# Own buffers for the first chunk's raw weights, and a running sum made by accumulating DMAs, in a two-layer encoder

## The chip, the cores and the metric

The kernel runs on one core of a Trainium2 chip. The metric is the time of one launch on the device, in microseconds (us). Below, PE is TensorE, DVE is VectorE, ACT is ScalarE, POOL is GpSimd and SP is SyncE. SP issues the loads; an engine name with a q behind it (SPq) is that engine's queue of DMA issues.

## The reference

Two layers are run on one sequence of 256 tokens of width 2048. Each layer multiplies x by a wide matrix, gives the columns to four attention branches (A to D), and adds the branches up, each with its own gate:

```python
x = _layer_norm(x, emb_ln_g, emb_ln_b)
for l in range(DEPTH):                      # DEPTH = 2
    h = jnp.einsum('bsd,de->bse', x, w_in)  # q, k, v, z of four branches, and gl
    ...
    ys = jnp.stack([ya * jax.nn.silu(az), yb * jax.nn.silu(bz), yc * jax.nn.silu(cz), yd * jax.nn.silu(dz)], axis=2)
    proj = jnp.einsum('bsnw,nwd->bsnd', ys, w_branch)
    gates = jax.nn.sigmoid(gl + b_gate).reshape(b, s, N_BRANCH, D_MODEL)
    merged = jnp.sum(proj * gates, axis=2)
    out = jnp.einsum('bsd,de->bse', merged, w_out)
    x = _layer_norm(DN_ALPHA * x + out, ln_g, ln_b)
```

## The kernel before

**Tiling.** The 256 tokens are two halves of 128 partitions. Weights come as raw groups of 128 x 1024 fp32 (512 KB, two k-tiles of 512 columns) in tiles `wraw` of a pool of four. ACT rounds a group to `whi` (line 145) and DVE takes the rest, `wlo` (line 146). A chunk of 512 columns is eight groups: PE multiplies each group three times (low x by high w, high x by high w, high x by low w; lines 190, 191 and 194) into one PSUM bank for each half. `chunk_t` (lines 217 and 218) does the same with the weights as the stationary side.

**The order of the work.** Each engine runs its own list in order. A scheduler makes the lists from the program's order and the free tiles; inside `first_chunk` the order is written out by hand. A wait at the head of an engine's list holds everything behind it.

**The first chunk.** `first_chunk` overlaps the first layer norm with the first 512 columns. x is loaded into `merged`, normalized, transposed on PE (line 558), scaled by ACT into `xt` or `xt1` (line 561) and split by ACT and DVE into `tx` (lines 235 and 236). For half 0, PE multiplies `xt` by the raw weights (`plain`, line 595, four matmuls of fp32 for each c). For half 1 it uses the split ones: `split_pass(c)` (lines 602, 603 and 606) reads two groups and the four k-tiles of `tx` that `x1_t(c)` has made. The eight raw groups are called raw 0 to raw 7 here. Raws 4 to 7 are issued one by one, each when `split` has freed a tile of the pool. Groups 4 to 7 are split into borrowed tiles (`wsp`, by `SPARE`). Behind raw 7 SP issues nine small loads (`small_weights`: rope tables, masks, `lp`, `sg`, `gn`), and only then the raw groups of the next chunk.

**The sum over the branches.** `gates(b)` runs over four chunks c of 512 columns: the gate's columns, then `gt` and `g` (lines 824 and 826), then a projection chunk of four groups, and then, for each half, `gp` = (g + 1) x projection (line 839) and `merged += gp` (line 840), both on DVE. Branch 0 writes `merged` directly (line 836). Around the last projection chunk, (b, c) = (3, 3), PE transposes columns c = 0, 1 and 2 of `merged` (line 806, `merged_t`). Columns c = 3 follow in `merged_last`, a task that is stepped after the first group of the first `w_out` chunk. `merged_t` fills `tx` again, the left side of that matmul.

Of the kernel before, what the change touches and what calls it, by code (L numbers as in the profile page):

```python
# [11 lines left out]
F32 = mybir.dt.float32  # L12
F32R = mybir.dt.float32r
AF = mybir.ActivationFunctionType
ALU = mybir.AluOpType
AX = mybir.AxisListType

P = 128
# [4 lines left out]
NK = D // P  # L23
KG = 2
# [2 lines left out]
TCH = 256  # L27

SPARE = [None] * 4 + [(("qkT", 3), ("qkT", 3)), (("v", 2), ("v", 2)), (("ra", 1), ("rb", 1)), (("yl", 2), ("yl", 2))]
NCH = 512  # L30
WARM = 40
ALPHA = (2 * DEPTH) ** 0.25
# [60 lines left out]
def hybrid_encoder(ctx: ExitStack, tc: tile.TileContext, a: dict, out: bass.AP):  # L93
# [33 lines left out]
    def load_bc(dst, src_1d):  # L127
        nc.sync.dma_start(out=dst, in_=src_1d.rearrange("(o n) -> o n", o=1).to_broadcast([P, src_1d.shape[0]]))

    loads = []  # L130


    def load_raw(src, off, w):
        raw = wrw.tile([P, KG * NCH], F32, tag="wraw", name="wraw")[:, :w]
        loads.append(nc.sync.dma_start(out=raw, in_=src[off:off + P * w].rearrange("(p m) -> p m", p=P)).ins)
        return raw

# [94 lines left out]
    def split_evac(hi, lo, src, scale=None):  # L232

        if scale is None:
            nc.scalar.copy(hi, src)
            nc.vector.tensor_tensor(out=lo, in0=src, in1=hi.bitcast(F32), op=ALU.subtract)  # L236
        else:
            nc.scalar.activation(out=hi, in_=src, func=AF.Copy, scale=scale)
            nc.vector.scalar_tensor_tensor(out=lo, in0=src, scalar=scale, in1=hi.bitcast(F32), op0=ALU.mult, op1=ALU.subtract)
# [327 lines left out]
    def first_chunk(src, off):  # L567

        acc = acc_banks()
        xt = cst.tile([P, NK, P], F32, tag="bias", name="xt")  # L570
        size = P * KG * NCH
        raws, ws = [], []

        def load_raws(n):
            for _ in range(n):
                raws.append(load_raw(src, off + len(raws) * size, KG * NCH))

        def split(n):
            for _ in range(n):
                g = len(ws)  # L580
                ws.append(split_w(raws[g], NCH, SPARE[g]))
                if g + 4 < NK // KG:
                    load_raws(1)

        def x0_t(c):
            x_t(0, c, xt[:, 4 * c:4 * c + 4])

        def x1_t(c):
            t = vec.tile([P, 4, P], F32, tag="tmp", bufs=3, name="xt1")
            x_t(1, c, t)  # L590
            x_split(1, c, t)

        def plain(c):
            for k in range(4 * c, 4 * c + 4):
                nc.tensor.matmul(acc[0], lhsT=xt[:, k], rhs=raws[k // KG][:, k % KG * NCH:(k % KG + 1) * NCH], start=k == 0, stop=k == NK - 1)  # L595

        def split_pass(c):
            for g in (2 * c, 2 * c + 1):
                hi, lo = ws[g]
                for kk in range(KG):  # L600
                    k = g * KG + kk
                    nc.tensor.matmul(acc[1], lhsT=tok(tl, k, 1, False), rhs=hi[:, kk], start=k == 0, stop=False)
                    nc.tensor.matmul(acc[1], lhsT=tok(th, k, 1, False), rhs=hi[:, kk], start=False, stop=False)
                for kk in range(KG):
                    k = g * KG + kk
                    nc.tensor.matmul(acc[1], lhsT=tok(th, k, 1, False), rhs=lo[:, kk], start=False, stop=k == NK - 1)

        load_x(0)
        nc.scalar.dma_start(out=gT, in_=a["emb_ln_gT"])
        nc.scalar.dma_start(out=bT, in_=a["emb_ln_bT"])  # L610
        load_raws(2)
        load_x(1)
        load_raws(2)

        idle = psa.tile([P, NCH], F32, tag="pa", name="idle")
        for _ in range(WARM):
            nc.tensor.transpose(idle[:, :P], ident, ident)
        m0 = stats_of(0)
        for c in range(4):
            center(0, c, *m0)  # L620
        split(1)
        x0_t(0)
        x0_t(1)
        split(1)
        m1 = stats_of(1)
        plain(0)
        x0_t(2)
        split(1)
        plain(1)
        x0_t(3)  # L630
        split(1)
        plain(2)
        for c in range(4):
            center(1, c, *m1)
        split(1)
        x1_t(0)
        split(1)
        plain(3)
        x1_t(1)
        split(1)  # L640
        split_pass(0)
        split(1)
        x1_t(2)
        split_pass(1)
        x1_t(3)
        split_pass(2)
        x_split(0, 0, xt[:, 0:4])
        x_split(0, 1, xt[:, 4:8])
        split_pass(3)
        x_split(0, 2, xt[:, 8:12])  # L650
        x_split(0, 3, xt[:, 12:16])
        return acc
# [18 lines left out]
    for l in range(DEPTH):  # L671
# [51 lines left out]
        def columns_ab(br):  # L723
            zs, ysT = new_branch()
            for u in range(2):
                v = v_tile()
                first = (br, u) == ("A", 0)
                if first and l == 0:
                    with tc.manual_schedule(engines={mybir.EngineType.PE, mybir.EngineType.Activation, mybir.EngineType.DVE, mybir.EngineType.SP}):
                        ps = first_chunk(w_in, OFFSETS[f"{br}vz{u}"])  # L730
                else:
                    ps = cols(f"{br}vz{u}", apart=first)
                if not sw:
                    if l == 0:
                        with tc.issue_after(loads[-1]):
                            sw.extend(small_weights())
                    else:
                        sw.extend(small_weights())
                neglam, sg, gn, bias = sw
                for half in range(2):  # L740
                    nc.vector.tensor_copy(v[:, half, 0:256], ps[half][:, 0:256])
                    silu2(ps[half][:, 256:512], zs[:, half, u * 256:(u + 1) * 256], sg if br == "A" else None)
                hi, lo = qkT_tile(4), qkT_tile(4)
                for b in range(2):
                    bs = slice(b * NCH, (b + 1) * NCH)
                    ps = cols_t(f"{br}qk{u}", b)
                    src = att.tile([P, 1024], F32, tag="ra", name="xr", bufs=1)[:, :NCH]
                    fold(ps, src.rearrange("p (n t) -> p n t", n=2))
                    if br == "A":
                        table = [rope_a[:, i].rearrange("p (j m) -> p j m", j=2).unsqueeze(1).to_broadcast([P, 2, 2, P]) for i in range(2)]  # L750
                        rotate(src.rearrange("p (n j m) -> p n j m", n=2, j=2), P, *table)
                    split_evac(hi[:, bs], lo[:, bs], src)
                tasks.append(attend_a(u, (hi, lo), v, zs, ysT, neglam) if br == "A" else attend_b(u, (hi, lo), v, zs, ysT, bias))
            if br == "A" and l == 0:
                tasks.append(keep_x())
            return ysT
# [57 lines left out]
        def gates(b, ysT, first):  # L814
            yh, yl = ysT
            for c in range(4):
                cs = slice(c * NCH, (c + 1) * NCH)
                bg = vec.tile([P, NCH], F32, tag="bc", name="bg")
                load_bc(bg, a["b_gate"][l][b * D + c * NCH:b * D + (c + 1) * NCH])
                ps = cols(f"G{b}{c}")  # L820
                gs = []
                for half in range(2):
                    t = vec.tile([P, NCH], F32, tag="tmp", bufs=3, name="gt")
                    nc.vector.tensor_tensor(out=t, in0=ps[half], in1=bg, op=ALU.add)  # L824
                    g = vec.tile([P, NCH], F32, tag="g", bufs=3, name="g")
                    nc.scalar.activation(out=g, in_=t, func=AF.Tanh, scale=0.5)  # L826
                    gs.append(g)
                if c == 0:
                    drain_for(b)
                if (b, c) == (3, 3):  # L830
                    for done in range(3):
                        merged_t(done)
                pp = chunk(w_br, (b * 4 + c) * P * 4 * NCH, NCH, 4, yh, yl)
                for half in range(2):
                    if first:
                        nc.vector.scalar_tensor_tensor(out=merged[:, half, cs], in0=gs[half], scalar=1.0, in1=pp[half], op0=ALU.add, op1=ALU.mult)
                    else:
                        t = vec.tile([P, NCH], F32, tag="tmp", bufs=3, name="gp")
                        nc.vector.scalar_tensor_tensor(out=t, in0=gs[half], scalar=1.0, in1=pp[half], op0=ALU.add, op1=ALU.mult)
                        nc.vector.tensor_tensor(out=merged[:, half, cs], in0=merged[:, half, cs], in1=t, op=ALU.add)  # L840

        pending = {}

# [144 lines left out]
```

## Time and profile before

| what | value |
|---|---|
| time, median of 3 runs | 2127.93 us (2125.24 to 2128.4) |
| the profiled execution, its own time | 2127.32 us |
| its span, first to last instruction | 2125.2 us |
| granted PE clock, mean | 0.997 |
| PE busy | 2105.6 us, 99% |
| DVE, ACT, POOL busy | 1316.8, 997.9 and 33.7 us |
| DMA, bytes moved and mean rate | 410.38 MB, 193 GB/s |

The time holds 2.1 us around the span. A busy PE is counted from pipelined matmuls, so that 99% says that PE hardly ever waits, not that it is at its peak. A chain of waits through the program is 97% PE.

### The profile page before, as it was taken

The page shows a single profiled execution, that of the slowest core. Times are in us where ns is not written, and L with a number is a line of the kernel's source. Part 1 is how long each engine was busy: PE and PEld are TensorE (multiplying, and loading weights), DVE is VectorE, ACT ScalarE, POOL GpSimd, SP SyncE. Part 2 cuts the span into 40 slices and gives each one's busy share as a digit, 9 for nine tenths or more (in the row PEclk, how much of TensorE's full clock was granted, in tenths as well). Part 3 has the DMA queues.
Part 4 walks back from the last instruction along what each step waited for, and adds up shares of the span by engine and source line. Part 5 has one row for each costly group of instructions (what it writes and reads, how often), then busy time and mean ns, then how long its engine had stood idle before and what let it go on. Part 6 is the DMA issues. An engine that isn't in the chain of part 4 may idle for free.

```text
span 2125.2 us, 27271 instructions
## 1 busy us (share of the span) xinstructions
PE 2105.6 (99%) x10480; PEld 1787.3 (84%) x10480; DVE 1316.8 (62%) x1635; ACT 997.9 (47%) x1335; POOL 33.7 (2%) x34
## 2 busy tenths in 40 slices
PE   8999999999999999999999999999999999999997
PEld 6888888888898988888888888888889999888886
DVE  6767655765566655556676665556656666555566
ACT  5654444444455544444446544444445454444442
POOL 1000100000000000000000000000000000000000
PEclk9999999999999999999999999999999999999999
DMA  7557566556555566666665555665565555666664
GB/s 245 180 179 264 194 201 195 185 182 198 181 175 169 171 206 204 212 198 225 204 211 181 173 169 189 199 187 187 184 203 183 174 168 179 196 200 214 198 217 145
DMA packets 121457, 410.38 MB, mean 193 GB/s; under 512 B 13872, under 2 KB 14896, under 8 KB 120816
## 3 DMA queue, kind: packets, MB, share of 16 engines
q1 hardware_dynamic: 120464, 407.59, 59.8%
q8 instruction: 82, 1.34, 0.3%
q10 hardware_dynamic: 864, 1.07, 0.1%
q14 instruction: 47, 0.39, 0.1%
HBM read 402.31 MB, written 6.29 MB: 192 GB/s over the span
## 4 chain that ended last, share of the span: by engine, by line
PE 97%; DVE 1%; DMA 1%; ACT 0%; issue 0%; DVEq 0%; POOL 0%; SPq 0%
PE pw L190 23%; PE pw L191 23%; PE pw L194 23%; PE pw L217 14%; PE pw L218 7%; PE pt L291 1%; PE po L446 1%; PE po L518 1%; PE sc L504 1%; DMA wraw<-in_w_in 0%; PE pw L595 0%; DVE wlo L146 0%; PE sc L378 0%; PE pt L806 0%; PE po L401 0%; PE pt L338 0%
## 5 line engine op out<-in xcount | busy, mean ns | idle before, releaser
L146 DVE TENSOR_TENSOR wlo<-wraw,whi 128x1024 fp32r<-128x1024 f32 (+1 forms) x720 | 865.8, 1204 | 653.1 <-ACT whi L145 653.0
L145 ACT CAST whi<-wraw 128x1024 fp32r<-128x1024 f32 (+1 forms) x720 | 742.7, 1033 | 930.3 <-PE pw L191 686.5
L190 PE MATMUL pw<-whi,tx 128*128 128x512 f32 (+1 forms) x1968 | 760.7, 387 | 0.4 <-DVE tx L236 0.4
L191 PE MATMUL pw<-whi,tx 128*128 128x512 f32 (+1 forms) x1968 | 753.6, 383 | 0.0
L194 PE MATMUL pw<-wlo,tx 128*128 128x512 f32 (+1 forms) x1968 | 593.3, 383 | 0.0
L217 PE MATMUL pw<-tx,whi 128*128 128x512 f32 x1280 | 457.0, 400 | 0.0
L190 PEld LDWEIGHTS pw<-whi,tx 128*128 128x128 f32 x1968 | 371.6, 189 | 65.9 <-DVE tx L236 0.6
L191 PEld LDWEIGHTS pw<-whi,tx 128*128 128x128 f32 x1968 | 371.8, 189 | 64.3
L194 PEld LDWEIGHTS pw<-wlo,tx 128*128 128x128 f32 x1968 | 368.6, 189 | 68.0
L218 PE MATMUL pw<-tx,wlo 128*128 128x256 f32 x1280 | 358.4, 280 | 0.0
L217 PEld LDWEIGHTS pw<-tx,whi 128*128 128x128 f32 x1280 | 240.4, 188 | 56.2
L218 PEld LDWEIGHTS pw<-tx,wlo 128*128 128x128 f32 x1280 | 241.7, 189 | 0.5
L190 PE MATMUL pw<-whi,yl 128*128 128x512 f32 x256 | 100.8, 394 | 0.0
L191 PE MATMUL pw<-whi,yh 128*128 128x512 f32 x256 | 99.8, 390 | 0.0
L194 PE MATMUL pw<-wlo,yh 128*128 128x512 f32 x256 | 79.4, 390 | 0.0
L194 PEld LDWEIGHTS pw<-wlo,yh 128*128 128x128 f32 x256 | 48.1, 188 | 10.1
L190 PEld LDWEIGHTS pw<-whi,yl 128*128 128x128 f32 x256 | 48.1, 188 | 9.6
L191 PEld LDWEIGHTS pw<-whi,yh 128*128 128x128 f32 x256 | 48.1, 188 | 9.5
L824 DVE TENSOR_TENSOR gt<-pw,bg 128x512 f32<-128x512 f32 x64 | 44.0, 687 | 9.4 <-PE pw L194 9.4
L826 ACT ACTIVATE g<-gt 128x512 f32<-128x512 f32 x64 | 37.2, 623 | 7.7 <-DVE gt L824 7.7
L325 ACT COPY xs<-qkT 32x512 f32<-32x512 f32 x48 | 29.7, 619 | 23.5 <-DVE qkT L230 23.2
L226 ACT COPY fo<-pw 128x256 f32<-128x256 f32 x80 | 29.7, 371 | 17.4 <-PE pw L218 17.2
(151 smaller groups left out, 1109.0 us busy)
## 6 DMA issues: line engine op xcount, KB each, us to landing
wraw<-in_w_in SPq DMA_DIRECT2D x544, 512.0 KB, 3.9
wraw<-in_w_branch SPq DMA_DIRECT2D x64, 512.0 KB, 3.4
wraw<-in_w_out SPq DMA_DIRECT2D x64, 512.0 KB, 4.3
wraw<-in_w_in SPq DMA_DIRECT2D x64, 384.0 KB, 3.1
bg<-in_b_gate SPq DMA_DIRECT2D x32, 256.0 KB, 4.3
xr<-x_dram SPq DMA_DIRECT2D x16, 256.0 KB, 4.7
bias<-in_rpb SPq DMA_DIRECT2D x2, 1024.0 KB, 6.7
x_dram<-merged SPq DMA_DIRECT2D x8, 256.0 KB, 5.1
```

The costliest lines, as they stand in the source:

```text
L145: nc.scalar.copy(hi[:, :w], raw)
L146: nc.vector.tensor_tensor(out=lo[:, :w], in0=raw, in1=hi[:, :w].bitcast(F32), op=ALU.subtract)
L190: nc.tensor.matmul(acc[half][:, :n], lhsT=tok(ll, k, half, perm), rhs=hi[:, kk, :n], start=k == 0, stop=False)
L191: nc.tensor.matmul(acc[half][:, :n], lhsT=tok(lh, k, half, perm), rhs=hi[:, kk, :n], start=False, stop=False)
L194: nc.tensor.matmul(acc[half][:, :n], lhsT=tok(lh, k, half, perm), rhs=lo[:, kk, :n], start=False, stop=k == nkt - 1)
L217: nc.tensor.matmul(acc[b], lhsT=hi[:, kk, cs], rhs=tx[:, k].rearrange("p h t -> p (h t)"), start=k == 0, stop=False)
L218: nc.tensor.matmul(acc[b][:, SEQ:], lhsT=lo[:, kk, cs], rhs=th[:, k, :], start=False, stop=k == NK - 1)
L226: nc.scalar.copy(t[:, b], acc[b][:, :SEQ])
L291: nc.tensor.transpose(pt[:, q * P:(q + 1) * P], src[:, q * P:(q + 1) * P], ident)
L325: nc.scalar.copy(xs[r:r + 32], x[r ^ 32:(r ^ 32) + 32])
L824: nc.vector.tensor_tensor(out=t, in0=ps[half], in1=bg, op=ALU.add)
L826: nc.scalar.activation(out=g, in_=t, func=AF.Tanh, scale=0.5)
```

## The change

Two things change. Raws 4, 5 and 6 get tiles of their own (`FIRST_RAW`, borrowed from the tags `zs`, `yh` and `qkT`), so all eight loads are asked for at the start and only raw 7 waits for a tile of the pool; the nine small loads are also tied by order behind the last split of x (`marks`). And `merged += gp` is no instruction of DVE: POOL issues a DMA that reads `gp` and adds it to `merged` in SBUF, 24 in each layer.

```diff
+FIRST_RAW = {4: ("zs", 2), 5: ("yh", 2), 6: ("qkT", 3)}
...
+    def load_raw(src, off, w, spare=None):
+        pl, tag, bufs = (wrw, "wraw", None) if spare is None else (ysp if spare[0] in ("zs", "yh") else att, *spare)
+        raw = pl.tile([P, KG * NCH], F32, tag=tag, name="wraw", **({"bufs": bufs} if bufs else {}))[:, :w]
...
-            nc.scalar.copy(hi, src)
-            nc.vector.tensor_tensor(out=lo, in0=src, in1=hi.bitcast(F32), op=ALU.subtract)
+            marks[:] = [nc.scalar.copy(hi, src).ins,
+                        nc.vector.tensor_tensor(out=lo, in0=src, in1=hi.bitcast(F32), op=ALU.subtract).ins]
...
-                raws.append(load_raw(src, off + len(raws) * size, KG * NCH))
+                g = len(raws)
+                raws.append(load_raw(src, off + g * size, KG * NCH, FIRST_RAW.get(g)))
...
                 ws.append(split_w(raws[g], NCH, SPARE[g]))
-                if g + 4 < NK // KG:
-                    load_raws(1)
...
-        load_raws(2)
+        load_raws(6)
...
-                        with tc.issue_after(loads[-1]):
+                        with tc.issue_after(loads[-1]), tc.issue_after(marks[0]), tc.issue_after(marks[1]):
...
                         nc.vector.scalar_tensor_tensor(out=t, in0=gs[half], scalar=1.0, in1=pp[half], op0=ALU.add, op1=ALU.mult)
-                        nc.vector.tensor_tensor(out=merged[:, half, cs], in0=merged[:, half, cs], in1=t, op=ALU.add)
+                        nc.gpsimd.dma_start(out=merged[:, half, cs], in_=t, accum_op=ALU.add)
```

The change also moves instructions. ACT's list in the first chunk, before (line numbers of the changed kernel are two or three higher; `xt1_299`, `_331` and `_355` belong to `x1_t(1)` to `x1_t(3)`; `whi_443`, `_465` and `_487` are the first three groups of the next chunk):

```order
L561 ACTIVATE xt1_299<-pt_300,bT_104,gT_103 128x128 x4
L235 CAST tx_99<-xt1_299 128x4x128
L145 CAST wsp_311<-wraw_246 128x1024
L145 CAST wsp_327<-wraw_265 128x1024
L561 ACTIVATE xt1_331<-pt_332,bT_104,gT_103 128x128 x4
L688 ACTIVATE le_411<-ls_409 128x2
L145 CAST whi_443<-wraw_441 128x1024
L235 CAST tx_99<-xt1_331 128x4x128
L561 ACTIVATE xt1_355<-pt_356,bT_104,gT_103 128x128 x4
L145 CAST whi_465<-wraw_463 128x1024
L235 CAST tx_99<-xt1_355 128x4x128
```

The same place on ACT after the change:

```order
L564 ACTIVATE xt1_299<-pt_300,bT_104,gT_103 128x128 x4
L148 CAST whi_443<-wraw_441 128x1024
L238 CAST tx_99<-xt1_299 128x4x128
L148 CAST wsp_311<-wraw_136 128x1024
L148 CAST wsp_327<-wraw_138 128x1024
L564 ACTIVATE xt1_331<-pt_332,bT_104,gT_103 128x128 x4
L148 CAST whi_465<-wraw_463 128x1024
L238 CAST tx_99<-xt1_331 128x4x128
L564 ACTIVATE xt1_355<-pt_356,bT_104,gT_103 128x128 x4
L148 CAST whi_487<-wraw_485 128x1024
L238 CAST tx_99<-xt1_355 128x4x128
```

Each cast of a next chunk's group stands one x-tile earlier, ahead of the cast of `xt1_299`; DVE's list has the matching `wlo` at the same places. PE's list in the first chunk is the same before and after.

PE's list at the end of layer 0's gates, before (`pw_8279` and `pw_8280` are the two halves of the first `w_out` chunk, `pt_8299` and `pt_8306` those of `merged_last`; in brackets the counters of the engines that an instruction waits for):

```order
L194 MATMUL pw_8280<-wlo_8284,tx_99 128x512 x2
L806 MATMUL pt_8299<-ident_87,merged_100 128x128 [waits DVE_49,PE_49]
L806 MATMUL pt_8299<-ident_87,merged_100 128x128 x3
L806 MATMUL pt_8306<-ident_87,merged_100 128x128 [waits DVE_49,PE_49]
L806 MATMUL pt_8306<-ident_87,merged_100 128x128 x3
L190 MATMUL pw_8279<-whi_8315,tx_99 128x512
L191 MATMUL pw_8279<-whi_8315,tx_99 128x512
```

The same place on PE after the change (DMASW are the counters of DMAs issued by POOL):

```order
L197 MATMUL pw_8280<-wlo_8284,tx_99 128x512 x2
L808 MATMUL pt_8299<-ident_87,merged_100 128x128 [waits DMASW6_49,DVE_49]
L808 MATMUL pt_8299<-ident_87,merged_100 128x128 x3
L193 MATMUL pw_8279<-whi_8315,tx_99 128x512
L194 MATMUL pw_8279<-whi_8315,tx_99 128x512
L808 MATMUL pt_8306<-ident_87,merged_100 128x128 [waits DMASW7_49,DVE_49]
L808 MATMUL pt_8306<-ident_87,merged_100 128x128 x3
```

The transposes of half 0 stand where they stood and now wait for a DMA; those of half 1 stand two matmuls later. In layer 1 the same rows come again.

## Rows read from the trace of the kernel before

**Rows 1.** The page's busy time of each engine, with share and instructions.

```profile
PE 2105.6 (99%) x10480; PEld 1787.3 (84%) x10480; DVE 1316.8 (62%) x1635; ACT 997.9 (47%) x1335; POOL 33.7 (2%) x34
```

**Rows 2.** The waits of PE, whole run: us in total, times, longest us.

```profile
PE pw L602 <- DVE tx L236: 3.0, 1, 3.0
PE pt L558 <- DVE merged L551: 2.7, 2, 1.9
```

**Rows 3.** Timeline of PE, 20 to 47 us: start, duration, [idle before <- releaser].

```profile
26.00 1.95 PE L595 MATMUL pw<-wraw,xt 128*128 128x512 f32 x4 [0.66 <-DMA wraw<-in_w_in]
...
31.36 0.50 PE L602 MATMUL pw<-whi,tx 128*128 128x512 f32 x1
...
34.21 0.60 PE L558 MATMUL pt<-ident,merged 128*128 128x128 f32 x4
...
45.00 0.39 PE L217 MATMUL pw<-tx,whi 128*128 128x512 f32 x1
```

**Rows 4.** Timeline of SP's DMA issues, 20 to 47 us.

```profile
22.53 0.33 SPq L135 DMA_DIRECT2D wraw<-in_w_in  x1
22.91 0.42 SPq L679 DMA_DIRECT2D rope_a<-in_rope_a  x1
...
27.81 12.54 SPq L135 DMA_DIRECT2D wraw<-in_w_in  x6
```

**Rows 5.** Timeline of ACT, 15 to 47 us.

```profile
28.43 1.50 ACT L561 ACTIVATE xt<-pt,bT,gT 128x128 f32<-128x128 f32 x4 [1.67 <-PE pt L558]
29.97 0.62 ACT L235 CAST tx<-xt 128x512 fp32r<-128x512 f32 x1
30.49 2.00 ACT L145 CAST wsp<-wraw 128x1024 fp32r<-128x1024 f32 x2
32.39 1.50 ACT L561 ACTIVATE xt<-pt,bT,gT 128x128 f32<-128x128 f32 x4
...
34.83 1.04 ACT L145 CAST whi<-wraw 128x1024 fp32r<-128x1024 f32 x1 [0.85 <-DMA wraw<-in_w_in]
35.78 0.61 ACT L235 CAST tx<-xt 128x512 fp32r<-128x512 f32 x1
36.30 1.50 ACT L561 ACTIVATE xt<-pt,bT,gT 128x128 f32<-128x128 f32 x4
37.68 1.05 ACT L145 CAST whi<-wraw 128x1024 fp32r<-128x1024 f32 x1
```

**Rows 6.** Busy time by stretch: PE, PEld, DVE, ACT, POOL, PE clock, DMA share, GB/s.

```profile
0.00:20.00 20.00, 16.70 (x76) 11.54 (x77) 11.28 (x20) 9.84 (x20) 2.72 (x8) 1.00 0.75 263
39.00:43.00 4.00, 4.00 (x12) 3.08 (x12) 4.00 (x7) 4.00 (x7) 0.00 (x0) 0.57 0.65 218
```

**Rows 7.** Timeline of all engines, 977 to 982.5 us, end of layer 0's gates.

```profile
977.71 0.68 DVE L839 SCALAR_TENSOR_TENSOR gp<-g,pw 128x512 f32<-128x512 f32 x1
...
977.98 0.62 PE L194 MATMUL pw<-wlo,yh 128*128 128x512 f32 x2
...
981.16 1.06 PE L806 MATMUL pt<-ident,merged 128*128 128x128 f32 x8
```

**Rows 8.** The same for 2025 to 2030 us, end of layer 1's gates.

```profile
2025.32 0.68 DVE L839 SCALAR_TENSOR_TENSOR gp<-g,pw 128x512 f32<-128x512 f32 x1
...
2028.77 1.06 PE L806 MATMUL pt<-ident,merged 128*128 128x128 f32 x8
```

**Rows 9.** The instructions of line 840, count and ns min/median/max.

```profile
L840 DVE TENSOR_TENSOR merged<-merged,gp x48: 682/687/694, 427.2 to 2028.4; 128x512 f32<-128x512 f32 x48
```

**Rows 10.** DMA issues in 970 to 990 us: count, KB each, median us to landing.

```profile
xr<-x_dram SPq DMA_DIRECT2D x3, 256.0 KB, 5.2
```

**Rows 11.** All DMAs of the tile `merged`, whole run.

```profile
DMA to landing us min/median/max: 2.5/4.9/6.3
```

**Rows 12.** Timeline of POOL, 5 to 20 us.

```profile
8.32 0.55 POOL L545 TENSOR_TENSOR rs<-ve,mhalf 128x1 f32<-128x1 f32 x1 [7.04 <-DVE ve L543]
18.24 1.48 POOL L545 TENSOR_TENSOR rs<-ve,mhalf 128x1 f32<-128x1 f32 x1 [9.37 <-DVE ve L543]
```

More of the change, by code (lines that the diff above doesn't have):

```diff
@@ L128, in load_bc @@
         nc.sync.dma_start(out=dst, in_=src_1d.rearrange("(o n) -> o n", o=1).to_broadcast([P, src_1d.shape[0]]))
-    loads = []
-    def load_raw(src, off, w):
-        raw = wrw.tile([P, KG * NCH], F32, tag="wraw", name="wraw")[:, :w]
+    loads, marks = [], []
+    def load_raw(src, off, w, spare=None):
+        pl, tag, bufs = (wrw, "wraw", None) if spare is None else (ysp if spare[0] in ("zs", "yh") else att, *spare)
+        raw = pl.tile([P, KG * NCH], F32, tag=tag, name="wraw", **({"bufs": bufs} if bufs else {}))[:, :w]
         loads.append(nc.sync.dma_start(out=raw, in_=src[off:off + P * w].rearrange("(p m) -> p m", p=P)).ins)
```

## The prediction

> **What bounds the kernel now.** I read the page first: PE is busy for 2105.6 of 2125.2 us, DVE for 62% [rows 1]. So work taken off DVE is worth nothing in itself, and only two things can move the time: the 20 us in which PE is idle, and new waits put into PE's list. The waits of PE come next [rows 2]: almost all of its idle time that something could be done about lies in the first chunk, 3.0 us before a `split_pass` that waits for an x-tile, and 2.7 us for the layer norm; 0.66 us for a raw weight stand in its timeline [rows 3]. Past the first chunk that view has no wait of PE as long as 0.5 us. So I read the timelines in two places: the first chunk, where the weights' loads change, and the end of the gates, where PE reads `merged` soonest after it is written.
>
> **The first chunk: what the loads give.** In before, SP issues raw 7 at 22.53, right ahead of the small loads, and PE waits 0.66 us for it until 26.00 [rows 3, 4]. With tiles of their own, raws 4 to 6 are asked for at once, and raw 7 as soon as the first pool tile is read, some 7 us sooner. So the 0.66 us goes, and the small loads and the next chunk's first group (`whi_443`'s raw) come sooner by the same: in before it is issued at 27.81, 4.9 us after the first small load [rows 4], and ACT has it at 34.83, after an idle 0.85 us [rows 5].
>
> What is late next is not a load but ACT and DVE, because the order shows each cast of the next chunk moved ahead of an x-tile. I walk it by start-to-start distances. PE reaches `x1_t(1)` 0.66 us sooner, so ACT's scaling starts at 28.43 - 0.66 = 27.77. From there [rows 5]: 1.54 us to its end (28.43 to 29.97), so `whi_443` at 29.31; 0.95 for a cast of weights (34.83 to 35.78), `tx` at 30.26; 0.52 (29.97 to 30.49), the two `wsp` casts at 30.78; 1.90 (30.49 to 32.39), the next scaling at 32.68; 1.38 (36.30 to 37.68), `whi_465` at 34.06; then `tx` of `x1_t(2)` at 35.01, the scaling of `x1_t(3)` at 35.53, and 1.38 later, allowing 0.3 for its transposes on PE, `whi_487` at 37.2.
>
> From such a `whi` to the `split_pass` behind it, DVE's `wlo` and `tx` included, before shows 34.83 to 37.79 = 2.96 us: the end of PE's 3.0 us wait, which began at 34.21 + 0.6 [rows 2, 3, 5]. So `split_pass(1)` starts at 29.31 + 2.96 = 32.27, a little later than before's 31.36; a pass takes 31.36 to 34.21 = 2.85 us [rows 3], so it ends at 35.1; `split_pass(2)` starts at 34.06 + 2.96 = 37.0, not 37.79; and `split_pass(3)` at 37.2 + 2.96 = 40.1, ending at 43.0. In before the chunk ended at 45.00 [rows 3]. **The gain is 2.0 us.**
>
> Most of that hangs on the clock. After the wait of 2.97 us the granted clock was 0.57 of full over 39 to 43 [rows 6], that is, for most of this stretch PE ran at 1.2 instead of 2.4 GHz; it cost 4 x 0.43 = 1.7 us. The longest wait for the layer norm, 1.9 us [rows 2], lies in the first 20 us, where the clock is 1.00 [rows 6]: no fall. The new waits are two, of about 1.6 us (`split_pass(0)` and the next transposes are done at about 30.7) and 1.5 us, so shorter than 1.9; I take it that the clock holds. If it falls, the gain is 0.3 us. So 0.3 to 2.0.
>
> The moved `lpp`, `ls`, `le` and `neglam` cost nothing: they are used only after the chunk's end, where PE has three finished groups of the next chunk. If that cover were gone, their 0.2 to 0.3 us each on DVE and ACT would show.
>
> **The running sum: what goes.** 48 DVE additions of 0.687 us [rows 9], 33 us of DVE. PE covers all of it, so 0.
>
> **The running sum: what comes.** POOL issues 24 DMAs for each layer; each reads 256 KB of `gp`, reads and writes 256 KB of `merged`. Behind them in POOL's list stands only the layer norm's power, due long after. In all branches but the last, the next reader of a sum comes at least a gate chunk later. A pass of two groups for one half takes 2.85 us [rows 3], so eight groups for both halves take 8 x 2.85 = 23 us, and behind those the landing is hidden, and so is the return of the three `tmp` tiles. The same holds for c = 0 to 2 of branch 3. The weights share the DMA engines with 12.6 MB more, 3% of the 410 MB moved before (6% if the second read counts); the four raw tiles cover that.
>
> What is not hidden is c = 3 of branch 3. `gp` of half 0 ends at 977.71 + 0.68 = 978.39 and PE stands at the transposes at 981.16: there are **2.77 us** [rows 7]. In layer 1 it is 2028.77 - 2026.00, again 2.77 [rows 8]. In before the addition took 0.69 of that. Now a DMA has to be issued, moved and landed in it. For half 1, the projection ends at 978.60 [rows 7], so `gp` at 979.29; it is wanted some 0.9 us after half 0's transposes, and does not wait again if it lands 0.9 us after half 0.
>
> No row shows a DMA of POOL or one that adds. The nearest is a load of the same size in these very microseconds, `xr`, 256 KB, 5.2 us from issue to landing [rows 10]; DMAs of `merged` take 2.5 to 6.3 us, 4.9 in the middle [rows 11]. The issue itself is POOL's work; its shortest instruction on a column takes 0.55 us, the longer one 1.48 [rows 12]. I take 5.2 + 0.55 = 5.75 us, a wait of 5.75 - 2.77 = **2.98 us for each layer**. Below: 2.5 + 0, no wait. Above: 6.3 + 1.48 = 7.78, a wait of 5.0.
>
> The Trainium skill prices such a DMA lower: "DMA: Bandwidth & Descriptors", section "Anatomy of one DMA — SWDGE (gpsimd) path", gives 2.0 us and the bytes at 436 GB/s, for 256 KB an estimate of 2.6 us; it would land in time, and the sum by it would be 2125.3. The quiet DMAs of `merged` agree with that (2.5) [rows 11], those beside the weights do not, and the second read is not in it.
>
> **The sum** is made on the profiled execution: 2127.32 - 2.0 + 2 x 2.98 = **2131.3 us**. The median of the runs shown is 2127.93, 0.6 above that execution. What a measurement here can tell from no change is about 0.2%, 4.3 us, so 2131.3 lies just inside "the same".
>
> **The rivals.**
>
> *The DMA lands in time.* For it: 2.5 us in a quiet stretch. Against: SP has an `xr` and weights under way at that moment. It decides at 2.77 us. Then nothing is lost and 2127.3 - 2.0 = 2125.3. This ends within 0.2%.
>
> *The clock falls in the new wait, or the DMA is longer.* This ends slower. PE's wait of 2.98 us is as long as the one of 2.97 after which the clock fell, though the work around it is denser. One fall costs 1.7 [rows 6]: 2133.0; two, 2134.7; with a landing of 7.78 us in both layers, 2127.3 - 2.0 + 10 + 3.4 = 2138.8, or 2140.5 if the first chunk loses its clock as well. It decides at a landing of about 6.2 us without a fall, 5.4 with one.
>
> *POOL is held up by DVE when it issues.* The same power took 0.55 us at 8.32, and 1.48 at 18.24 while DVE was splitting weights [rows 12]. `gp` of half 1 and a `wlo` run on DVE right when POOL has to issue. If both issues of the layer's last pair lose that 0.93 us, the half that ends last is 1 to 1.9 us later: 2133.3 to 2135.1. Of this the Trainium skill has a rule, "SBUF — State Buffer", section "Who interferes with whom": a DVE instruction in a mode with two ports locks GpSimd out until it ends. The trace shows the stretching, not its cause.
>
> *The first chunk gains nothing.* ACT now asks for the next chunk's first group at 29.31. If the small loads still stand in the way and it lands after 31.3, `split_pass(1)` loses what the later passes gain: 2133.3.
>
> **How the numbers follow.** The forecast, landings of 5 to 6.3 us and the first chunk's gain, gets 0.40 (2129 to 2133; a fifth of it above 2132.2, where slower begins). In time: 0.20. Clock or longer landing: 0.26. POOL held up: 0.07. No gain at the start: 0.04. Faster by over 0.2% would need 4.3 us out of a first chunk that offers 2.0: 0.03. Same is 0.32 + 0.20 = 0.52; slower 0.08 + 0.26 + 0.07 + 0.04 = 0.45; faster 0.03. The range goes from just above the case in time, 2126, to 2139, the long landing with two falls.
>
> **What would show it.** In the changed profile: no wait of PE for `wraw`; two waits before `split_pass(1)` and `(2)` of about 1.5 us each, `chunk_t` starting near 43.0 at full clock; `merged`'s DMAs of POOL landing 5 to 6 us after their issue; PE's longest new waits just before the transposes of `merged_last`, some 3 us in each layer, named as waits for a DMA; DVE's busy time down by 33 us and no wait for `tmp`. Wrong would be: landings below 3 or above 6.5 us, a clock below 1 after the transposes, or PE waiting anywhere else in the gates.

## The result and the profile after

| | before | after |
|---|---|---|
| median, us | 2127.72 (4 runs) | 2142.2 (4 runs, 2140.15 to 2142.8) |
| profiled execution / its span, us | 2127.32 / 2125.2 | 2142.8 / 2140.9 |
| mean granted clock | 0.997 | 0.995 |

The ratio is 1.007, 95% interval 1.0058 to 1.0082: slower by 14.5 us, outside the range of 2126 to 2139, and past the 0.2% that tells a change from none. The page's busy line and the waits of PE (us in total, times, longest) after:

```profile
PE 2109.8 (99%) x10480; PEld 1789.5 (84%) x10480; DVE 1290.3 (60%) x1587; ACT 998.4 (47%) x1335; POOL 77.0 (4%) x82
```

```profile
PE pt L808 <- DMA merged<-gp: 11.6, 3, 5.7
PE pw L604 <- DVE tx L239: 2.5, 2, 1.3
...
PE pt L341 <- DVE ys L453: 1.3, 1, 1.3
PE pt L808 <- DVE tx L242: 0.5, 1, 0.5
```

Against [rows 1, 2]: DVE is relieved, the 3.0 us wait is two shorter ones, and the sum's DMA has become PE's largest wait.

Both traces hold the same 10,480 matmuls in nearly the same order, so the start of each in after, less its start in before, tells where the time went (times of before):

| up to | first chunk's end | 258 us | 266 | 974 | 1000 | 2022 | end |
|---|---|---|---|---|---|---|---|
| after - before, us | -2.64 | -2.74 | -1.20 | -1.24 | 6.47 | 6.42 | 15.63 |

So the change gains 2.64 us in the first chunk and loses 1.54 near 263 us, 7.71 at the end of layer 0's gates and 9.21 at the end of layer 1's, with no more than 0.1 us anywhere between. On the profiled execution: 2127.32 + 15.6 = 2142.9, and it took 2142.8.

**First chunk.** Timeline of PE after, as in [rows 3]:

```profile
31.63 0.50 PE L604 MATMUL pw<-whi,tx 128*128 128x512 f32 x1 [1.19 <-DVE tx L239]
...
36.38 0.50 PE L604 MATMUL pw<-wsp,tx 128*128 128x512 f32 x1 [1.27 <-DVE tx L239]
...
39.51 0.50 PE L604 MATMUL pw<-wsp,tx 128*128 128x512 f32 x1
...
42.36 0.39 PE L220 MATMUL pw<-tx,whi 128*128 128x512 f32 x1
```

**End of the gates.** `gp` of DVE (half 0, half 1) and the two issues of POOL, layer 0:

```profile
976.48 0.68 DVE L841 SCALAR_TENSOR_TENSOR gp<-g,pw 128x512 f32<-128x512 f32 x1
977.41 0.69 DVE L841 SCALAR_TENSOR_TENSOR gp<-g,pw 128x512 f32<-128x512 f32 x1 [0.25 <-PE pw L197]
977.46 1.80 POOL L842 DMA_DIRECT2D merged<-gp  x2 [26.59 <-DVE gp L841]
```

PE behind them, layer 0 and then layer 1 (compare [rows 7, 8], where all eight transposes stand together without a wait):

```profile
979.47 0.61 PE L197 MATMUL pw<-wlo,tx 128*128 128x512 f32 x2
985.49 1.09 PE L808 MATMUL pt<-ident,merged 128*128 128x128 f32 x4 [5.40 <-DMA merged<-gp]
986.23 0.78 PE L193 MATMUL pw<-whi,tx 128*128 128x512 f32 x1
...
987.98 1.09 PE L808 MATMUL pt<-ident,merged 128*128 128x128 f32 x4 [0.55 <-DVE tx L242]
...
989.24 0.40 PE L194 MATMUL pw<-whi,tx 128*128 128x512 f32 x1
...
2034.74 0.61 PE L197 MATMUL pw<-wlo,tx 128*128 128x512 f32 x2
2041.04 1.09 PE L808 MATMUL pt<-ident,merged 128*128 128x128 f32 x4 [5.69 <-DMA merged<-gp]
...
2043.47 1.09 PE L808 MATMUL pt<-ident,merged 128*128 128x128 f32 x4 [0.49 <-DMA merged<-gp]
...
2046.91 0.57 PE L193 MATMUL pw<-whi,tx 128*128 128x512 f32 x1
2047.33 0.39 PE L194 MATMUL pw<-whi,tx 128*128 128x512 f32 x1
```

In layer 0, half 0 is there 985.49 - 977.16 = 8.3 us after its `gp` ended, half 1 987.98 - 978.10 = 9.9 us after its own; in layer 1 8.6 and 10.1. (In layer 0 the view names DVE's `tx` before half 1, since that `tx`, of half 0, ended at 987.93. In layer 1 the same transposes start at 2043.47 and the same `tx` ended at 2043.48, so they do not wait for it. The DMA is what came: in all four cases the transposes start 0.14 us behind its landing.) Between the two halves PE has only half 0's transposes and two matmuls to do. At half clock they last 1.94 us, where full clock takes about 0.95, so the 0.5 us in the view hides most of the second wait.

The same stretches by windows (PE, PEld, DVE, ACT, POOL, PE clock, DMA share, GB/s), and DMA queues and landings over 976 to 990 us (queue rows: packets, MB, share of 16 engines; issues: count, KB each, median us to landing):

```profile
980.00:984.00 4.00, 0.09 (x1) 0.00 (x0) 1.23 (x1) 0.76 (x1) 0.00 (x0) 0.79 0.99 226
984.00:988.00 4.00, 1.96 (x7) 1.30 (x7) 0.69 (x1) 0.60 (x1) 0.00 (x0) 0.50 1.02 333
...
2044.00:2048.00 4.00, 4.00 (x13) 3.23 (x12) 0.69 (x1) 0.85 (x2) 0.00 (x0) 0.59 0.03 10
```

```profile
q1 hardware_dynamic: 863, 2.62, 57.8%
q0 software_dynamic: 288, 0.52, 20.4%
...
merged<-gp POOLq DMA_DIRECT2D x2, 256.0 KB, 8.7
xr<-x_dram SPq DMA_DIRECT2D x2, 256.0 KB, 9.4
```

The DMA engines are full (1.0) while PE is idle, and `xr`, 5.2 us in [rows 10], takes 9.4 in layer 0. The clock is 0.50 behind the wait, that is 1.2 GHz: matmuls stand 0.43 us apart, and 0.23 again from 989.2 and from 2047.3.

**Near 263 us**, POOL's addition of the mask to the bias, DVE's splits of weights, and PE (three timelines):

```profile
255.91 5.76 POOL L705 TENSOR_TENSOR bias<-bias,mask_b 128x1024 f32<-128x1024 f32 x2 [82.48 <-DMA bias<-in_rpb]
```

```profile
256.07 6.69 DVE L149 TENSOR_TENSOR wlo<-wraw,whi 128x1024 fp32r<-128x1024 f32 x2 [1.97 <-ACT whi L148]
262.68 0.60 DVE L453 SCALAR_TENSOR_TENSOR ys<-po,rdp,zs 128x128 f32<-128x128 f32 x2
```

```profile
263.08 0.59 PE L341 MATMUL pt<-ident,ys 128*128 128x128 f32 x3 [1.26 <-DVE ys L453]
```

Two `wlo` take 6.69 us instead of 2 x 1.23, `ys` comes late, and PE waits for it. One by one, the additions end at 258.32 and 261.68 and the splits at 259.40 and 262.76: each split ends 1.1 us behind an addition, about its own length, as if it had run only once that one was done.

### The profile page after: what moved, and what is told of

Read it like the earlier page. It is cut to its first block, busy times and chain, and to the rows that moved or that the text cites. A ratio compares the mean times of both kernels' runs of the same rounds, so it can differ in the third digit from the quotient of the medians.

```text
span 2140.9 us, 27417 instructions
## 1 busy us (share of the span) xinstructions
PE 2109.8 (99%) x10480; PEld 1789.5 (84%) x10480; DVE 1290.3 (60%) x1587; ACT 998.4 (47%) x1335; POOL 77.0 (4%) x82
## 4 chain that ended last, share of the span: by engine, by line
issue 48%; PE 46%; POOL 2%; DVE 2%; DMA 1%; ACT 1%; DVEq 0%; POOLq 0%; SPq 0%
PE pw L193 12%; PE pw L194 11%; PE pw L197 11%; PE pw L220 6%; PE pw L221 3%; POOL merged L842 2%; DMA merged<-gp 1%; DVE wlo L149 1%; PE po L449 0%; PE pw L597 0%; PE pt L294 0%; PE sc L381 0%; PE po L404 0%; DMA merged<-in_x 0%; ACT xt L564 0%
## 5 line engine op out<-in xcount | busy, mean ns | idle before, releaser
L842 POOL DMA_DIRECT2D merged<-gp x48 | 41.8, 886 | 1103.8 <-DVE gp L841 1075.5
L197 PEld LDWEIGHTS pw<-wlo,yh 128*128 128x128 f32 x256 | 48.1, 188 | 10.1
```

The source lines that it names most:

```text
L197: nc.tensor.matmul(acc[half][:, :n], lhsT=tok(lh, k, half, perm), rhs=lo[:, kk, :n], start=False, stop=k == nkt - 1)
L842: nc.gpsimd.dma_start(out=merged[:, half, cs], in_=t, accum_op=ALU.add)
```

## The experiments

My theory after the result: the loss is the last pair's landing, long because SP's loads share the DMA engines with it, and the clock that falls behind the wait. The rivals: the addition itself is slow; or POOL's issue is.

### Which part costs: each alone

**loads_only**: the first chunk's part alone.

```diff
-nc.gpsimd.dma_start(out=merged[:, half, cs], in_=t, accum_op=ALU.add)
+nc.vector.tensor_tensor(out=merged[:, half, cs], in0=merged[:, half, cs], in1=t, op=ALU.add)
```

> The changed kernel with the running sum back on DVE, so the first chunk's part of the change stands alone. If the loss lies at the two layers' ends (my theory, and both rivals on the landing), this gives the first chunk's 2.6 us and loses at most the 1.5 us seen near 263 us: 2125.3 to 2126.8, no wait of PE for merged. If the loss near 263 us belongs to the accumulating DMAs, the 1.5 us is gone here and the gain is 2.6; if it belongs to the loads, 1.1 is left.

Measured 2125.16 us, ratio to before 0.9987 (0.9978 to 0.9996). The first chunk gives 2.51, 0.35 is lost near 263 us, nothing at the layers' ends.

**sum_only**: the kernel before with the other half of the diff alone.

```diff
-nc.vector.tensor_tensor(out=merged[:, half, cs], in0=merged[:, half, cs], in1=t, op=ALU.add)
+nc.gpsimd.dma_start(out=merged[:, half, cs], in_=t, accum_op=ALU.add)
```

> The kernel before with the accumulating DMAs alone, without the first chunk's buffers. If the two parts add up, as my theory has it, this is the changed kernel without its 2.6 us at the start: 15.5 to 18.5 us above the kernel before, 2143.5 to 2146. If the earlier loads of the change are what brings the collision about (near 263 us or at the layers' ends), it is less than 13 us.

Measured 2144.51, ratio 1.0081 (1.0066 to 1.0096), 17.1 us above the kernel before: 8.0 at the end of layer 0, 9.2 at the end of layer 1. The parts add up, and the early loads do not bring the loss at the ends about.

### Is it the one pair, or all 48 DMAs

**last_on_dve**: 44 of the 48 DMAs stay.

```diff
-nc.gpsimd.dma_start(out=merged[:, half, cs], in_=t, accum_op=ALU.add)
+if (b, c) == (3, 3):
+    nc.vector.tensor_tensor(out=merged[:, half, cs], in0=merged[:, half, cs], in1=t, op=ALU.add)
+else:
+    nc.gpsimd.dma_start(out=merged[:, half, cs], in_=t, accum_op=ALU.add)
```

> The changed kernel, but the last chunk of the last branch (c = 3, b = 3) is added by DVE; 22 accumulating DMAs for each layer stay. If all of the loss at the layers' ends comes from the landing of that one pair, the 7.7 - 1.5 and 9.2 - 7.7 and what the clock lost behind them go: 14.2 us less than the changed kernel, some 2126 to 2128, and no stretch at half clock at 982 and 2040 us. If the other 22 DMAs cost something too (the third tmp tile, the shared DMA engines, POOL), more than 2 us above the kernel before are left, and PE shows waits in the gates.

Measured 2124.82, ratio 0.9988 (0.9979 to 0.9997). Nothing is lost at either end; the other 44 DMAs, with their 11.6 MB (421.94 against 410.38 moved), cost nothing.

**later_read**: all 48 stay, and PE reads the last quarter later.

```diff
 def merged_last():
+    for _ in range(4):
+        yield
     merged_t(3)
```

> The changed kernel, with the transposes of the last quarter of merged put four steps later in PE's list, behind more groups of the first w_out chunk; nothing is left out. The landing itself stays as it is (8 to 10 us by my theory and by both rivals), but PE has 6 to 11 us of other work ahead of it: if the wait alone is the loss, it shrinks from 5.4 to under 2 us, the clock holds, and the time falls by 10 to 14 us, to 2128 to 2132. If the time stays near 2142, the loss is not in that wait.

Measured 2124.93, ratio 0.9986 (0.9977 to 0.9995), below the 2128 to 2132 that I expected. PE's timeline, and the landings over 960 to 1002 us:

```profile
990.43 1.03 PE L808 MATMUL pt<-ident,merged 128*128 128x128 f32 x8
```

```profile
merged<-gp POOLq DMA_DIRECT2D x2, 256.0 KB, 9.1
```

The landing is as long as ever, the transposes stand without a wait, and 17 us are gone: a landing of 9 us costs nothing where PE has other work that long.

### What makes the landing long

**loads_away**: `xr` and the layer norm's weights are asked for behind the `w_out` raws.

```diff
-gb = norm_weights(a["ln_g"][l], a["ln_b"][l])
...
-    xr = []
-    for half in range(2):
-        t = vec.tile([P, NCH], F32, tag="g", bufs=3, name="xr")
-        nc.sync.dma_start(out=t, in_=x_dram[l][half * P:(half + 1) * P, cs])
-        xr.append(t)
     ps = chunk(w_out, c * NK * P * NCH, NCH, NK, th, tl, apart=c == 3)
+    xr = []
+    with tc.issue_after(loads[-3]):
+        for half in range(2):
+            t = vec.tile([P, NCH], F32, tag="g", bufs=3, name="xr")
+            nc.sync.dma_start(out=t, in_=x_dram[l][half * P:(half + 1) * P, cs])
+            xr.append(t)
+        if c == 1:
+            gb = norm_weights(a["ln_g"][l], a["ln_b"][l])
```

> The changed kernel, with the loads of xr and of the layer norm's weights issued behind the w_out raws instead of right beside the last pair of accumulating DMAs; nothing is left out. If the landing of 8.3 to 9.8 us comes from sharing the DMA engines with these loads (my theory), it falls to 5 to 6.5 us, the wait to 2 to 3.5, and the time by 5 to 12 us. If it comes from the read and write of each accumulated piece, or from POOL's own issue, the landing stays above 8 us and the time near 2142.

Measured 2139.0, ratio 1.0054 (1.004 to 1.0067): only 3 us better, although the landing fell as my theory had it. Landings of 960 to 1002 and of 2010 to 2055 us, then loads over 974.35 to 988.35 us (which stands to this run's `gp` as 976 to 990 does to that of after), and PE at both ends:

```profile
merged<-gp POOLq DMA_DIRECT2D x2, 256.0 KB, 5.8
...
merged<-gp POOLq DMA_DIRECT2D x2, 256.0 KB, 6.2
```

```profile
q1 hardware_dynamic: 576, 1.84, 37.5%
...
xr<-x_dram SPq DMA_DIRECT2D x1, 256.0 KB, 3.9
```

```profile
980.88 0.63 PE L808 MATMUL pt<-ident,merged 128*128 128x128 f32 x4 [2.45 <-DMA merged<-gp]
...
983.50 1.09 PE L808 MATMUL pt<-ident,merged 128*128 128x128 f32 x4 [1.52 <-DMA merged<-gp]
...
2034.97 0.63 PE L808 MATMUL pt<-ident,merged 128*128 128x128 f32 x4 [2.20 <-DMA merged<-gp]
2038.86 1.09 PE L808 MATMUL pt<-ident,merged 128*128 128x128 f32 x4 [2.80 <-DMA merged<-gp]
```

This is the case that I had forecast: half 0 is there 5.4 and 5.1 us after its `gp`, waits of 2.45 and 2.20. Still 6.8 and 7.5 us are lost, since half 1 comes 2.6 and 3.9 us behind half 0, and the clock falls even here. The edit takes only a part of the loads away: 1.84 MB of loads against 2.62 still move in these 14 us, one `xr` is still issued 0.3 us ahead of the pair, and the DMA engines are still full from 979 to 983 us (share 1.06).

**plain_copy** and **copy_away**: POOL's DMAs overwrite `merged`, so the sum over the branches is left out; the second has the loads away too.

```diff
-nc.gpsimd.dma_start(out=merged[:, half, cs], in_=t, accum_op=ALU.add)
+nc.gpsimd.dma_start(out=merged[:, half, cs], in_=t)
```

> The changed kernel with the same 48 DMAs from POOL, but without the addition: each overwrites its part of merged, so the sum over the branches is left out. If reading and writing each piece for the addition is a good part of the landing, the landing of the last pairs falls from 8.3 to 9.8 us to 6 or less, and their packets take less time on the DMA engines. If the landing comes from POOL's issue or from the loads beside it alone, it stays above 8 us and the time within 2 us of 2142.

> The two earlier edits together: POOL's DMAs overwrite merged instead of adding to it (the sum over the branches is left out), and xr's and the layer norm's loads are issued behind the w_out raws. If the loads beside it and the addition each lengthen the landing by themselves, the landing of the last pairs falls from 5.8 and 6.2 us (loads away, with the addition) to 4 to 5 us. If only one of them matters at a time, it stays at 5.8 or above.

One run each: 2138.01 and 2132.68. Queue and landings over 960 to 1002 us of plain_copy, then the landings of copy_away (its queue row is the same):

```profile
q0 software_dynamic: 160, 0.52, 3.1%
...
merged<-gp POOLq DMA_DIRECT2D x2, 256.0 KB, 6.9
```

```profile
merged<-gp POOLq DMA_DIRECT2D x2, 256.0 KB, 4.7
```

In plain_copy the landing of 6.9 lies between the two outcomes that I had written down, in copy_away it is as expected.

| median landing of the last pair, layers 0 / 1, us | loads beside it | part of the loads away |
|---|---|---|
| adding | 8.7 / 8.9 | 5.8 / 6.2 |
| overwriting | 6.9 / 7.0 | 4.7 / 4.3 |
| **lost at the two ends together, us** | | |
| adding | 16.9 | 14.3 |
| overwriting | 13.5 | 7.4 |

So both count: the loads that were moved 2.2 to 2.9 us of landing, the addition 1.1 to 1.9. The cells are single executions; in the four other runs that leave the pair as it is in after, it took 8.3 to 9.4, so a cell is good to about half a microsecond. The theory was one part of it, and the first rival is another. The adding pair goes out in 288 packets, the overwriting one in 160 for the same 0.52 MB; in after they took 20.4% of 16 engines over 14 us, 46 us, here 3.1% over 42, 21 us. POOL's issue, too, is shorter without the addition (0.55 us for a DMA, 0.89 with it), so some of the 1.1 to 1.9 us is the issue's. What stays, 4.3 to 4.7 us, holds the rest of the issue and the loads that were not moved, and no run took either away alone; it is still too long for the 2.77 us that there are.

### What the clock costs

**fill_wait** and **fill_more**: transposes of the identity in PE's wait.

```diff
 def merged_last():
+    fill = psa.tile([P, NCH], F32, tag="pa", name="fill")
+    for _ in range(32):
+        nc.tensor.transpose(fill[:, :P], ident, ident)
     merged_t(3)
```

```diff
 for half in range(2):
+    if c == 3:
+        fill = psa.tile([P, NCH], F32, tag="pa", name="fill")
+        for _ in range((52, 22)[half]):
+            nc.tensor.transpose(fill[:, :P], ident, ident)
     pt = psa.tile([P, NCH], F32, tag="pa", name="pt")
```

> The changed kernel with 32 more transposes of the identity, 5.5 us of PE's time by the warm-up's 40 in 6.90 us, put into the wait ahead of the last quarter's transposes in each layer; their result is not used, and nothing is left out. They end about when the sum lands, so the wait stays in the time but PE is never idle. If the clock's fall is a part of the loss of its own (my theory: 1.8 us in the first layer, 3.1 in the second), the granted clock stays at 2.4 GHz and the time falls by 4 to 5 us from 2142.2, to about 2137.5. If the wait is all, the time stays within 1 us of 2142.

Measured 2144.91, ratio 1.0079 (1.0066 to 1.0093). I had sized the filler wrongly, as PE's timeline shows:

```profile
978.64 3.65 PE L815 MATMUL fill<-ident 128*128 128x128 f32 x32
984.31 0.63 PE L808 MATMUL pt<-ident,merged 128*128 128x128 f32 x4 [2.01 <-DMA merged<-gp]
```

It took 3.65 us, the clock fell all the same, and the projection's two matmuls no longer stood between the halves. On the clock this run decides nothing by itself.

> The changed kernel with 52 transposes of the identity ahead of half 0's last transposes and 22 between half 0's and half 1's, 5.9 and 2.5 us by the 32 in 3.65 us that were too few; their result is not used, nothing is left out. They cover both waits, so PE is not idle until the sum has landed. If the clock's fall is a loss of its own (my theory), no stretch at 1.2 GHz is left at 982 and 2040 us and the time falls by 2 to 5 us from 2142.2, less than the 4.9 us counted at half clock, since the projection's first two matmuls no longer lie between the halves. If the wait is all of the loss, it stays at 2142 or above.

Measured 2140.98, ratio 1.0066 (1.0049 to 1.0083). Its windows, PE's timeline around half 1 of each layer, and the landing of half 1 (issued at 976.79 and at 2032.37):

```profile
980.00:984.00 4.00, 4.00 (x39) 4.00 (x37) 0.42 (x1) 0.00 (x0) 0.00 (x0) 1.00 1.07 286
984.00:988.00 4.00, 4.00 (x36) 3.87 (x35) 0.69 (x1) 1.12 (x2) 0.00 (x0) 1.00 0.68 245
...
2040.00:2044.00 4.00, 3.63 (x32) 3.62 (x33) 0.69 (x1) 0.73 (x2) 0.00 (x0) 1.00 0.58 217
```

```profile
986.84 0.60 PE L812 MATMUL pt<-ident,merged 128*128 128x128 f32 x4
...
2043.23 0.60 PE L812 MATMUL pt<-ident,merged 128*128 128x128 f32 x4
```

```profile
merged<-gp POOLq DMA_DIRECT2D x1, 256.0 KB, 9.1
...
merged<-gp POOLq DMA_DIRECT2D x1, 256.0 KB, 9.9
```

PE is kept busy, the clock stays at 1.00, and yet the ends lose 8.1 and 8.9 us against 7.7 and 9.2. Two things hide the gain. The filler was too long: half 1 had landed at 985.9 and 2042.3, and PE took it up some 0.8 us later in each layer than the 0.14 us that after shows. And the filler takes the place of the two matmuls between the halves, 0.54 us in each layer. Half 1's two landings are as long in sum as in after (19.0 us from issue, 19.1 there), so without these two the ends would lose about 16.9 - 1.6 - 1.1 = 14.2 us at full clock, an estimate, against 16.9 in after: the clock cost about 2.7 us. My reckoning of 4.9 us does not stand: most of the half-clock microseconds lay inside the wait for half 1 and cost nothing more. What can cost is the half clock behind half 1's transposes: (989.2 - 987.98)/2 = 0.6 and (2047.3 - 2043.47)/2 = 1.9, together 2.5.

### What happens near 263 us

**bias_dve**: loads_only, with the mask added to the bias by DVE, just before its first use.

```diff
-nc.gpsimd.tensor_tensor(out=bv, in0=bv, in1=mask_b.unsqueeze(1).to_broadcast([P, 16, GRID_W]), op=ALU.add)
...
+if u == 0:
+    for i in range(2):
+        bv = bias[:, i].rearrange("p (n c) -> p n c", c=GRID_W)
+        nc.vector.tensor_tensor(out=bv, in0=bv, in1=mask_b.unsqueeze(1).to_broadcast([P, 16, GRID_W]), op=ALU.add)
```

> The first chunk's part alone (the sum on DVE), and the masked bias added by DVE, just before its first use, instead of by POOL. If POOL's addition is what stretches the two splits of weights near 256 to 262 us (4.99 us for the two in the first chunk's part alone), each takes 1.23 us there and PE has no wait near 263 us: 0.3 us less than 2125.2. If the stretching has another cause, a wlo of 2 us or more is still to be seen there. As a version it should beat both kernels, by a little.

Measured 2124.69, ratio 0.9988 (0.9979 to 0.9997). DVE's timeline:

```profile
254.38 2.35 DVE L464 TENSOR_TENSOR bias<-bias,mask_b 128x1024 f32<-128x1024 f32 x2
256.65 1.22 DVE L149 TENSOR_TENSOR wlo<-wraw,whi 128x1024 fp32r<-128x1024 f32 x1
259.17 1.23 DVE L149 TENSOR_TENSOR wlo<-wraw,whi 128x1024 fp32r<-128x1024 f32 x1 [1.30 <-ACT whi L148]
```

Without POOL's addition every `wlo` is back at 1.23 us, and nothing is lost there: shown. With it the loss was 1.54 in after, 0.86 in last_on_dve, 0.85 in copy_away, 0.35 in loads_only, 0.08 in fill_wait, and 0.0 in later_read, loads_away, plain_copy and fill_more. It goes by how soon before the first of the two `wlo` the bias lands: 0.3 us in after, 1.0 in last_on_dve and copy_away, 1.5 in loads_only, 1.7 in fill_wait, 1.9 or more in the runs without a loss. sum_only, without the early loads, loses nothing there; its bias is asked for at 251.1 us, in the runs with them at 248.4 to 249.8. So the risk comes with the early loads, and the size is a draw of each execution. Of the versions tried, loads_only, last_on_dve, later_read and this one beat the kernel before, by 0.12 to 0.14%, and cannot be told apart.

## Why the prediction was wrong, step by step

**Right.** The first chunk: forecast 2.0 us, measured 2.64 (1.8 to 3.0 over the runs that have it). The walk gave `split_pass(1)` to `(3)` at 32.27, 37.0 and 40.1 and the chunk's end at 43.0; they came at 31.63, 36.38, 39.51 and 42.36, so the whole chain 0.6 us sooner than I had it, with the distances of the walk, the clock at 1.00 and the two waits shorter (1.19 and 1.27). The size is good to about a microsecond only: in sum_only, whose first chunk is that of before, it ended 0.94 us sooner than in the trace of before. Also right: a typical adding DMA, 5.9 us to landing where I said 5 to 6; nothing for DVE's 33 us; and nothing for the 44 DMAs that have work behind them. All 48 of after:

```profile
DMA to landing us min/median/max: 3.5/5.9/9.7
```

**The step that failed** is "a wait of 5.75 - 2.77 = 2.98 us for each layer", in three places. Let half 1's landing be counted from its `gp`'s end to its transposes. PE is busy for 1.99 us of it (978.10 to 980.09), and 0.41 of half 0's transposes and 0.54 of two projection matmuls fill a little more, 2.94 in all (loads_only takes 0.82 for all eight transposes and 0.54 for the two matmuls, at full clock). Then the loss is the landing less 2.94, and half of the stretch at half clock behind it. Half clock ends at 989.2 and 2047.3 in after, at 988.7 and 2043.4 in loads_away, at 991.0 and 2049.2 in fill_wait (where it begins behind half 1, at 987.6, in layer 0); fill_more has none at the ends. With a filler the two matmuls do not stand between the halves, and 2.40 is taken off:

| | landing of half 1 | less 2.94 or 2.40 | half clock | sum | measured |
|---|---|---|---|---|---|
| after, layer 0 | 9.88 | 6.94 | 0.6 | 7.5 | 7.71 |
| after, layer 1 | 10.11 | 7.17 | 1.9 | 9.1 | 9.21 |
| loads_away, layer 0 | 7.06 | 4.12 | 2.6 | 6.7 | 6.76 |
| loads_away, layer 1 | 8.08 | 5.14 | 2.3 | 7.4 | 7.52 |
| fill_wait, layer 0 | 10.10 | 7.70 | 1.7 | 9.4 | 9.39 |
| fill_wait, layer 1 | 10.43 | 8.03 | 2.5 | 10.5 | 10.51 |
| fill_more, layer 0 | 10.35 | 7.95 | 0 | 8.0 | 8.05 |
| fill_more, layer 1 | 11.15 | 8.75 | 0 | 8.8 | 8.85 |

So the account holds to 0.2 us in eight cases, with the clock's term where the clock fell and without it where it did not. (In fill_more, 0.8 us of each landing is the filler's.) Against the prediction:

1. The landing of half 0, forecast at 5.75 from an `xr` row, was 8.3 and 8.6. The `xr` row was no fair stand-in: the pair carries twice its bytes, its packets cost the DMA engines 46 us where overwriting ones cost 21, and the loads beside it are slowed as well (`xr` 9.4 in layer 0). Even my upper bound of 7.78 was too low.
2. Half 1 "does not wait again if it lands 0.9 us after half 0". It landed 2.4 to 2.5 us after half 0, and the half that comes last sets the time. This spoils the forecast even where half 0 lands as I said: in loads_away half 1 alone makes it 4.1 and 5.1 us, before any clock, where I had 2.98.
3. The sum had no fall of the clock at the ends; only a rival had. It fell in both layers; the 1.7 us that I gave for a fall is about what it cost in layer 1 (1.9), and in layer 0 it cost 0.6.

The rival "clock falls, or the DMA is longer" (0.26) was the right one, at 2133 to 2140.5; its upper end lacked half 1. Two of the prediction's own signs of being wrong showed: landings above 6.5 us, and a clock below 1 behind the transposes. That the DMA lands in time, the other rival, is far from every run. The Trainium skill, page "DMA: Bandwidth & Descriptors", section "Anatomy of one DMA — SWDGE (gpsimd) path", gave an estimate of 2.6 us for it. The trace does not agree for a DMA that adds: none of after took under 3.5 us, and the last pair took 4.3 to 4.7 even when it overwrote and part of the loads was out of its way. Only the quickest DMAs that overwrite came near the estimate, at 2.3. The measurement decides.

**The rival of POOL held up by DVE** turned round: POOL's issue started 0.3 us after `gp` and took 0.9 a DMA, so it was not held up; it was DVE that POOL stretched, near 263 us, in a place where I had looked for nothing. With this the Trainium skill agrees, "SBUF — State Buffer", section "Who interferes with whom": a DVE instruction with two SBUF inputs contends with a GpSimd instruction that reads SBUF, for a pair of ports that is an exclusive lock. `wlo` and the bias addition are such a pair, 6.69 us for two instead of 2.46. (The prediction quoted that section's rule for DVE modes with two ports; it is this neighbouring one that bears on a `wlo`.)

## What to carry to other kernels

Moving an addition from a half-idle engine to a DMA freed nothing here, and turned a 0.69 us dependence into one of 8 to 10 us where the next reader was near and loads ran beside it: do it only where the reader has that much other work, and keep the last piece on the engine (last_on_dve), or move the reader back (later_read). Price a transfer with what it will share the DMA engines with, count the last of the pieces that a reader needs rather than the first, and do not take a load's landing for that of a DMA that adds. A gain and a loss in one diff are worth separating: half of this one alone was worth 0.13%.

## What was not expected of the hardware

- A pair of DMAs that add went out in 288 packets where one that overwrites took 160 for the same 0.52 MB; it cost the DMA engines 46 instead of 21 us, and POOL 0.89 instead of 0.55 us for each issue.
- Of two such DMAs issued 0.9 us apart the second was used 2.4 to 3.9 us after the first.
- A shorter wait need not lose less by the clock: in loads_away, with PE back at work sooner, 4.9 us were lost behind half 1 at half clock, in after 2.5, by the table.
